# The order of the hand-over between stages: high-part passes first, sums in wide steps, nothing on GpSimd

## The chip, the cores and the metric

The kernel runs on one core of a Trainium2 chip. The time is the device time of one execution in microseconds (us); less is better. Three runs of the kernel before gave 1493.19, 1494.71 and 1496.35 us, median 1494.71.

## What is computed

A block of two transformer layers and a third, hybrid layer, for 256 tokens of width 1024 and 16 meta tokens put before them (272 tokens up to the last part of the second layer, 256 from there). In outline:

```python
for i in range(2):
    f1 = swiglu(rmsnorm(h, g[0]), w_gate, w_up, w_down);  h = h + 0.5 * rmsnorm(f1, g[1])
    m = attention(rmsnorm(h, g[2]));                       h = h + rmsnorm(m, g[3])   # neighborhood, then differential
    f2 = swiglu(rmsnorm(h, g[4]), ...);                    h = h + 0.5 * rmsnorm(f2, g[5])
x = x + rms_norm(concat(causal_attention, mlstm) @ w_out, g)    # its projections: rms_norm(x) @ w_in
x = x + rms_norm(square(relu(rms_norm(x, g) @ w_up)) @ w_down, g)
```

All is float32. Every stage is therefore the same in form: a norm of the residual h, products with large weights, some work between, a last product, and the norm of that added to h.

## The kernel before

h lies in SBUF with the features on the partitions, as eight blocks of 128 features by 272 tokens. Every product is made of three passes over parts in float32r: each weight chunk of 1024 by 128 is split in a high part `wh` and a low part `wl`, x in `xh` and `xl`, and TensorE adds `wh*xh + wh*xl + wl*xh` (`mm3`, lines 358 to 360). `gemm` makes one tile of 128 outputs: eight blocks of x, three matmuls each.

**Weights.** `Weights` streams raw chunks in by DMAs that SyncE issues (three buffers), `high()` copies a half to `wh` on ScalarE (L122), `low()` subtracts to `wl` (L134) on the engine that it is given, or else on `W.engine`, which is VectorE outside the mixers; when the second half of a raw chunk is through, the next load is issued. At most seven split chunks (`W_BUFS`) stand ready or in use. `pump(n)` makes up to n lows and highs; it is called behind every gemm.

**The end of a part.** `Post.evac` takes the eight last tiles: their squares into a sum, and `f = m*g`. `Post.finish` makes rstd: row sums on TensorE (L309, products with ones), a power on GpSimd (L314), and transposes back to columns (L333 to L338) into PSUM as `bc`. Then block j of the new residual is `h = h + f*bc`: `addend` (L561, `hb`, one operand in PSUM) and the addition (L567).

**The start of the next part.** `Norm` has x = h*g without rstd, which is applied behind the products: `block` makes `xh` on ScalarE (L401), `low` makes `xl` on VectorE (L411), `square` the squares on ScalarE (L344, L350, L352) and their sum `accp` on GpSimd (L353, L407). `head` makes the row sums of that sum and rstd, `tail` turns it (`rb`, L420); both run inside the second gemm behind the first tiles, `head` behind its block 0 and `tail` behind its block 3.

**The hand-over** is `start_phase`, called seven times: ahead of the three mixers, of three feed-forward parts, and of the last one (the first feed-forward has `first_phase`, with another order). While `finish` and its wait run, TensorE turns over on weights (`turn_over`, L433, two sets of nine). For blocks 0 and 1 `xh` is made straight from the addend (L442, from `old`, h*g of before, and `hb`), and h gets its addend beside that on GpSimd (L444). Then the first four tiles of the new stage are made together, block by block: for block k eight passes with `xh` (L455 and L456, L468 and L469) and four with `xl` (L459, L471), 96 matmuls in all; the low part of block k and the residual of block k + 2 stand in turn on VectorE, and two `W.pump(1, pool)` put two weight splits on GpSimd. Each engine works its queue in the order of the program.

Of the kernel before, what the change touches and what calls it, by code (L numbers as in the profile page):

```python
# [21 lines left out]
T = S + NM  # L22
# [51 lines left out]
class Weights:  # L74
    """Streams weight chunks [128, kb, 256] and splits each half of their columns into two
    float32r parts; of chunks with all their columns side by side, each half of their rows."""
# [64 lines left out]

    def pump(self, n=2, engine=None):
        ready = self.n_high
        for _ in range(n):
            if self.n_split < ready:
                self.low(engine)
            self.high()
        self.flush()
# [23 lines left out]
def block_kernel(ctx: ExitStack, tc: tile.TileContext, a, out):  # L172
# [25 lines left out]
    def keep_in(*slots):  # L198
        """The blocks that keep() hands out in turn during a mixer."""
        ring_blocks[:] = [t[:, j, :] for t in slots for j in range(t.shape[1])]  # L200
# [116 lines left out]
    def mean_head(acc, cols):  # L317
        """The mean of the squares, in rows of tokens."""
        p, m = ps_t((128, 4)), small([128, 4])
        n = row_sums(p, acc, cols)  # L320
        dve.tensor_scalar(m[:, 0:n], p[:, 0:n], 1.0 / D, EPS, op0=OP.mult, op1=OP.add)
        return m
# [18 lines left out]
    def square_into(acc, src, j, cols, bias=0.0, engine=dve):  # L341
        """The squares into the sum; the last block's stay beside it, for the product with ones."""
# [45 lines left out]
    class Norm:  # L388
        """x = h*g, split in two parts block by block; rstd is applied behind the products."""
# [18 lines left out]

        def low(self, j):
            c = self.cols  # L410
            dve.scalar_tensor_tensor(self.xl[:, j, c], h[:, j, c], self.g[:, j:j + 1],  # L411
                                     self.xh[:, j, c].bitcast(F32), op0=OP.mult, op1=OP.subtract)
# [10 lines left out]
    def start_phase(norm, post, n=4):  # L423
        """The first tiles, block by block of x as it comes.  The first two blocks of x are summed
        beside h, and the tensor engine turns over on weights while nothing is there for it."""
# [14 lines left out]
        t = [post.addend(k) for k in range(2)]  # L440
        for k in range(2):
            dve.scalar_tensor_tensor(norm.xh[:, k, c], t[k][:, c], norm.g[:, k:k + 1], old[k][:, c],  # L442
                                     op0=OP.mult, op1=OP.add)
            pool.tensor_tensor(h[:, k, c], h[:, k, c], t[k][:, c], op=OP.add)  # L444
        post.block(2)
        norm.block(2)
        norm.low(0)
        norm.low(1)
        post.block(3)
        norm.block(3)  # L450
        for k in range(2):
            norm.square(k)
        for k in range(2):
# [3 lines left out]
        for k in range(2):  # L457
            for q in range(n):
                pe.matmul(ps[q][:, c], w[q][0][:, k, :], norm.xl[:, k, c], start=False, stop=False)  # L459
        W.pump(1, pool)  # L460
        for k in range(2, 8):
            norm.low(k)
            if k + 2 < 8:
                post.block(k + 2)
                norm.block(k + 2)
            norm.square(k)
            for q in range(n):
                pe.matmul(ps[q][:, c], w[q][0][:, k, :], norm.xh[:, k, c], start=False, stop=False)  # L468
                pe.matmul(ps[q][:, c], w[q][1][:, k, :], norm.xh[:, k, c], start=False, stop=False)  # L469
            for q in range(n):  # L470
                pe.matmul(ps[q][:, c], w[q][0][:, k, :], norm.xl[:, k, c], start=False, stop=k == 7)  # L471
            if k == 5:
                W.pump(1, pool)
# [4 lines left out]
    def first_phase(norm, feed, n=4):  # L478
        """The first tiles of all: the passes in the order in which their operands come."""
# [53 lines left out]
    class Post:  # L533
        """The last products of a part: f = m*g beside the sum of squares, then h += f*rstd."""
# [96 lines left out]
    def proj_out(post, x, order=range(8)):  # L631
        """The product behind a mixer: the first four tiles block by block while the mixer ends."""
# [193 lines left out]
    def transpose_pair(dst, src):  # L826
        """[128, T] -> three token tiles, the last one with the last 16 tokens only."""
# [6 lines left out]
    class Ring:  # L834
        """Tiles of a mixer's turned weights, in the place of the residual's addend."""
# [10 lines left out]
    def softmax(ps, parts, n):  # L846
        """exp(logits - max) and 1/sum; the bias comes in parts of the columns."""
# [37 lines left out]
    def available(n):  # L885
        """Steps without work until the products have brought this unit's operands."""
# [200 lines left out]
    def token_rms(o):  # L1087
        """The sum of the squares of a token tile's 128 columns."""
# [422 lines left out]
    # the last product with the tokens on the partitions: out = h + (u @ w) * rstd * g  # L1511
# [90 lines left out]
```

## Time and profile before

| | |
|---|---|
| median of three runs | 1494.71 us |
| span of the profiled execution | 1495.0 us |
| TensorE busy | 1445.0 us (97%) |
| VectorE busy | 913.4 us (61%) |
| ScalarE busy | 753.9 us (50%) |
| GpSimd busy | 413.7 us (28%) |

PE is TensorE's matmuls, PEld its weight loads, DVE is VectorE, ACT is ScalarE, POOL is GpSimd. Records of neighbouring instructions can overlap, because the end of one is recorded after the next has begun: so the step from start to start, not the duration, tells the pace of a queue. A line in the timeline may stand for several like instructions in a row (x2), with the time from the first start to the last end; in brackets stand the idle time of the engine before it and what ended it.

### The profile page before, as it was taken

The page shows a single profiled execution, that of the slowest core. Times are in us where ns is not written, and L with a number is a line of the kernel's source. Part 1 is how long each engine was busy: PE and PEld are TensorE (multiplying, and loading weights), DVE is VectorE, ACT ScalarE, POOL GpSimd, SP SyncE. Part 2 cuts the span into 40 slices and gives each one's busy share as a digit, 9 for nine tenths or more (in the row PEclk, how much of TensorE's full clock was granted, in tenths as well). Part 3 has the DMA queues.
Part 4 walks back from the last instruction along what each step waited for, and adds up shares of the span by engine and source line. Part 5 has one row for each costly group of instructions (what it writes and reads, how often), then busy time and mean ns, then how long its engine had stood idle before and what let it go on. Part 6 is the DMA issues. An engine that isn't in the chain of part 4 may idle for free.

```text
span 1495.0 us, 27199 instructions
## 1 busy us (share of the span) xinstructions
PE 1445.0 (97%) x10996; PEld 1374.9 (92%) x10996; DVE 913.4 (61%) x1727; ACT 753.9 (50%) x1369; POOL 413.7 (28%) x300
## 2 busy tenths in 40 slices
PE   9999999899999999999999899999999898999998
PEld 8999998688899999999999798999999887999886
DVE  6777448853775544865545755675555667586542
ACT  5554445554664444554444565564444555576541
POOL 4324005452322100522102564232200855030000
PEclk9999999999999999999999999999999899999999
DMA  8896554432375555365553423276554533256651
GB/s 238 252 256 184 183 162 134 107 100 71 108 256 181 169 181 166 96 216 170 183 167 102 159 96 114 85 226 187 173 184 135 163 120 111 89 172 195 212 179 46
DMA packets 231708, 236.43 MB, mean 158 GB/s; under 512 B 17825, under 2 KB 221798, under 8 KB 231390
## 3 DMA queue, kind: packets, MB, share of 16 engines
q1 hardware_dynamic: 230750, 229.63, 49.2%
q0 software_dynamic: 688, 4.99, 1.1%
q8 instruction: 87, 1.43, 0.4%
q14 instruction: 39, 0.32, 0.1%
q10 hardware_dynamic: 144, 0.07, 0.0%
HBM read 233.60 MB, written 5.13 MB: 160 GB/s over the span
## 4 chain that ended last, share of the span: by engine, by line
PE 67%; DVE 7%; ACT 2%; issue 2%; POOL 1%; POOLq 0%; DVEq 0%; ACTq 0%
PE pm L358 18%; PE pm L360 18%; PE pm L359 18%; PE ps L1526 2%; PE ps L1525 2%; DVE xl L411 2%; PE ps L1527 2%; DVE h L567 1%; DVE hb L561 1%; PE ps L1129 1%; PE pt L309 1%; POOL accp L353 1%; PE ps L1101 1%; ACT wh L122 1%; PE ps L932 0%
## 5 line engine op out<-in xcount | busy, mean ns | idle before, releaser
L358 PE MATMUL pm<-xh,wh 128*128 128x272 f32 (+1 forms) x1992 | 584.4, 293 | 0.4 <-DVE s L851 0.4
L360 PE MATMUL pm<-xh,wl 128*128 128x272 f32 (+1 forms) x1992 | 572.6, 287 | 0.0
L359 PE MATMUL pm<-xl,wh 128*128 128x272 f32 (+1 forms) x1992 | 571.1, 287 | 0.0
L122 ACT ACTIVATE wh<-wr 128x1024 fp32r<-128x1024 f32 (+2 forms) x433 | 443.4, 1033 | 190.6 <-PE pm L359 119.4
L134 DVE TENSOR_TENSOR wl<-wr,wh 128x1024 fp32r<-128x1024 f32 (+1 forms) x354 | 444.7, 1262 | 130.4 <-ACT wh L122 129.5
L358 PEld LDWEIGHTS pm<-xh,wh 128*128 128x128 f32 x1992 | 378.6, 190 | 14.3 <-issue 11.1
L360 PEld LDWEIGHTS pm<-xh,wl 128*128 128x128 f32 x1992 | 378.3, 190 | 0.0
L359 PEld LDWEIGHTS pm<-xl,wh 128*128 128x128 f32 x1992 | 378.2, 190 | 0.1
L134 POOL TENSOR_TENSOR wl<-wr,wh 128x1024 fp32r<-128x1024 f32 x80 | 194.7, 2441 | 91.4 <-ACT wh L122 85.4
L360 PE MATMUL pm<-mh,wl 128*128 128x272 f32 (+1 forms) x704 | 202.3, 287 | 0.0
L358 PE MATMUL pm<-mh,wh 128*128 128x272 f32 (+1 forms) x704 | 202.1, 287 | 0.0
L359 PE MATMUL pm<-ml,wh 128*128 128x272 f32 (+1 forms) x704 | 201.5, 286 | 0.0
L594 POOL TENSOR_TENSOR sr<-sl,rb 128x272 f32<-128x272 f32 (+1 forms) x88 | 106.4, 1213 | 319.9 <-ACT sl L592 319.9
L360 PEld LDWEIGHTS pm<-mh,wl 128*128 128x128 f32 x704 | 132.7, 189 | 0.0
L358 PEld LDWEIGHTS pm<-mh,wh 128*128 128x128 f32 x704 | 132.6, 188 | 0.0
L359 PEld LDWEIGHTS pm<-ml,wh 128*128 128x128 f32 x704 | 132.6, 188 | 0.0
L314 POOL TENSOR_TENSOR s<-s,mhalf 128x3 f32<-128x3 f32 (+1 forms) x15 | 12.0, 799 | 386.0 <-DVE s L327 372.9
L385 ACT ACTIVATE mh<-m 128x272 fp32r<-128x272 f32 (+1 forms) x88 | 37.7, 428 | 120.4 <-DVE m L599 120.2
L599 DVE TENSOR_TENSOR m<-pm,sr 128x272 f32<-128x272 f32 (+1 forms) x88 | 38.2, 434 | 78.1 <-PE pm L360 70.5
L592 ACT ACTIVATE sl<-gq 128x272 f32<-128x272 f32 (+1 forms) x88 | 36.9, 428 | 87.9 <-DVE gq L590 87.5
L590 DVE TENSOR_TENSOR gq<-pm,rb 128x272 f32<-128x272 f32 (+1 forms) x88 | 37.5, 433 | 70.1 <-PE pm L360 62.2
L353 DVE TENSOR_TENSOR accf<-accf,sq 128x272 f32<-128x272 f32 (+1 forms) x42 | 18.3, 435 | 83.3 <-ACT sq L352 83.2
(345 smaller groups left out, 1998.9 us busy)
## 6 DMA issues: line engine op xcount, KB each, us to landing
wr<-in_ffn_w_gate_dram SPq DMA_DIRECT2D x43, 1024.0 KB
wr<-in_ffn_w_up_dram SPq DMA_DIRECT2D x43, 1024.0 KB
wr<-in_ffn_w_down_dram SPq DMA_DIRECT2D x32, 1024.0 KB
wr<-in_w_up_dram SPq DMA_DIRECT2D x16, 1024.0 KB
wr<-in_w_down_dram SPq DMA_DIRECT2D x16, 1024.0 KB
wr<-in_ffn_w_down_dram SPq DMA_DIRECT2D x16, 768.0 KB
wr<-in_na_w_qkv_dram SPq DMA_DIRECT2D x12, 1024.0 KB
wr<-in_da_w_qkv_dram SPq DMA_DIRECT2D x12, 1024.0 KB
```

The source lines that it names most:

```text
L122: self.nc.scalar.activation(hi, w, AF.Copy)
L134: engine.tensor_tensor(lo, w, hi.bitcast(F32), op=OP.subtract)
L353: engine.tensor_tensor(acc[:, cols], acc[:, cols], q[:, cols], op=OP.add)
L358: pe.matmul(ps, wh[:, k, :], xh[:, j, cols], start=start, stop=False)
L359: pe.matmul(ps, wh[:, k, :], xl[:, j, cols], start=False, stop=False)
L360: pe.matmul(ps, wl[:, k, :], xh[:, j, cols], start=False, stop=stop)
L385: act.activation(hi, src, AF.Copy)
L411: dve.scalar_tensor_tensor(self.xl[:, j, c], h[:, j, c], self.g[:, j:j + 1], self.xh[:, j, c].bitcast(F32), op0=OP.mult, op1=OP.subtract)
L590: dve.tensor_tensor(t[:, c], ps[:, c], norm.rb[:, c], op=OP.mult)
L592: act.activation(s[:, c], t[:, c], AF.Silu)
L594: pool.tensor_tensor(s2[:, c], s[:, c], norm.rb[:, c], op=OP.mult)
L599: dve.tensor_tensor(t[:, c], ps[:, c], gated.pop(f)[:, c], op=OP.mult)
```

## The change

In `start_phase` alone, with two small methods for it:

- The addends into h of blocks 0 and 1 go from GpSimd to VectorE, and behind the residual's other six blocks; `xh` of block 0 now stands ahead of the addend of block 1.
- VectorE makes the residual of all the blocks 2 to 7 before the first low part, then all eight low parts in a row. On TensorE all 64 passes with `xh` stand first and the 32 with `xl` behind.
- The squares are three wide instructions on ScalarE (blocks 2 to 5, 6 and 7, 0 and 1), into the place of the addends' factor f, with two weight copies (`W.high()`) between them. `Norm.sum` adds them on VectorE in three steps of 4, 2 and 1 blocks' width.
- The two weight splits that GpSimd had are `W.low_if()` on VectorE, one ahead of the sum and one behind it.

Comments and docstrings are taken out so that the line numbers stay.

```diff
+    def low_if(self):
+        if self.n_split < self.n_high:
+            self.low()
...
+        def sum(self, sq):
+            c = self.cols
+            dve.tensor_tensor(sq[:, 0:4, c], sq[:, 0:4, c], sq[:, 4:8, c], op=OP.add)
+            dve.tensor_tensor(sq[:, 0:2, c], sq[:, 0:2, c], sq[:, 2:4, c], op=OP.add)
+            dve.tensor_tensor(self.acc[:, c], sq[:, 0, c], sq[:, 1, c], op=OP.add)
...
-        t = [post.addend(k) for k in range(2)]
+        t = []
         for k in range(2):
+            t.append(post.addend(k))
             dve.scalar_tensor_tensor(norm.xh[:, k, c], t[k][:, c], norm.g[:, k:k + 1], old[k][:, c],
                                      op0=OP.mult, op1=OP.add)
-            pool.tensor_tensor(h[:, k, c], h[:, k, c], t[k][:, c], op=OP.add)
-        post.block(2)
-        norm.block(2)
-        norm.low(0)
-        norm.low(1)
-        post.block(3)
-        norm.block(3)
-        for k in range(2):
-            norm.square(k)
-        for k in range(2):
+        for k in range(2, 8):
+            post.block(k)
+            norm.block(k)
         for k in range(2):
+            dve.tensor_tensor(h[:, k, c], h[:, k, c], t[k][:, c], op=OP.add)
+        squares = post.f
+        for x, y in ((2, 6), (6, 8), (0, 2)):
+            act.activation(squares[:, x:y, c], h[:, x:y, c], AF.Square)
+            if x:
+                W.high()
+        for k in range(8):
+            norm.low(k)
+        for k in range(8):
             for q in range(n):
                 pe.matmul(ps[q][:, c], w[q][0][:, k, :], norm.xh[:, k, c], start=k == 0, stop=False)
                 pe.matmul(ps[q][:, c], w[q][1][:, k, :], norm.xh[:, k, c], start=False, stop=False)
-        for k in range(2):
-            for q in range(n):
-                pe.matmul(ps[q][:, c], w[q][0][:, k, :], norm.xl[:, k, c], start=False, stop=False)
-        W.pump(1, pool)
-        for k in range(2, 8):
-            norm.low(k)
-            if k + 2 < 8:
-                post.block(k + 2)
-                norm.block(k + 2)
-            norm.square(k)
-            for q in range(n):
-                pe.matmul(ps[q][:, c], w[q][0][:, k, :], norm.xh[:, k, c], start=False, stop=False)
-                pe.matmul(ps[q][:, c], w[q][1][:, k, :], norm.xh[:, k, c], start=False, stop=False)
+        for k in range(8):
             for q in range(n):
                 pe.matmul(ps[q][:, c], w[q][0][:, k, :], norm.xl[:, k, c], start=False, stop=k == 7)
-            if k == 5:
-                W.pump(1, pool)
+        W.low_if()
+        norm.sum(squares)
+        W.low_if()
         W.done(n)
         W.pump(2)
```

## Rows read from the trace of the kernel before

**Rows 1.** The page: span, and busy time (share of the span) and instructions by engine.

```profile
span 1495.0 us, 27199 instructions
PE 1445.0 (97%) x10996; PEld 1374.9 (92%) x10996; DVE 913.4 (61%) x1727; ACT 753.9 (50%) x1369; POOL 413.7 (28%) x300
```

**Rows 2.** Windows, product to row sums (one of seven): length, engines' busy, clock, DMA.

```profile
386.37:409.56 23.19, 20.79 (x158) 19.60 (x158) 17.59 (x27) 11.30 (x24) 14.26 (x12) 1.00 0.25 74
...
sum 157.56, PE 139.78 PEld 131.88 DVE 121.21 ACT 80.70 POOL 98.10; mean PE 19.97 PEld 18.84 DVE 17.32 ACT 11.53 POOL 14.01
```

**Rows 3.** Timeline of TensorE, hand-over from 386 us: start, length, line, tiles.

```profile
389.43 1.31 PE L433 MATMUL pm<-wh 128*128 128x256 f32 x9
391.32 0.39 PE L455 MATMUL pm<-xh,wh 128*128 128x272 f32 x1 [0.58 <-DVE xh L442]
...
399.85 0.77 PE L471 MATMUL pm<-xl,wh 128*128 128x272 f32 x4 [1.09 <-DVE xl L411]
...
405.37 0.28 PE L358 MATMUL pm<-xh,wh 128*128 128x272 f32 x1
...
408.40 0.29 PE L358 MATMUL pm<-xh,wh 128*128 128x272 f32 x1
...
409.56 0.83 PE L309 MATMUL pt<-ones,accp 128*128 128x1 f32 x6 [0.62 <-POOL accp L407]
```

**Rows 4.** Timeline of VectorE in the same hand-over.

```profile
389.62 0.79 DVE L561 TENSOR_TENSOR hb<-f,pt 128x272 f32<-128x272 f32 x2 [1.60 <-PE pt L335]
390.32 1.87 DVE L442 SCALAR_TENSOR_TENSOR xh<-hb,G,go 128x272 fp32r<-128x272 f32 x2
392.11 0.42 DVE L561 TENSOR_TENSOR hb<-f,pt 128x272 f32<-128x272 f32 x1
392.57 0.44 DVE L567 TENSOR_TENSOR h<-h,hb 128x272 f32<-128x272 f32 x1
392.93 0.91 DVE L411 SCALAR_TENSOR_TENSOR xl<-h,G,xh 128x272 fp32r<-128x272 f32 x2
...
397.26 2.53 DVE L411 SCALAR_TENSOR_TENSOR xl<-h,G,xh 128x272 fp32r<-128x272 f32 x1
...
404.67 3.38 DVE L134 TENSOR_TENSOR wl<-wr,wh 128x1024 fp32r<-128x1024 f32 x1 [0.77 <-ACT wh L122]
...
413.32 1.21 DVE L134 TENSOR_TENSOR wl<-wr,wh 128x1024 fp32r<-128x1024 f32 x1
```

**Rows 5.** Timeline of GpSimd in the same hand-over.

```profile
388.10 0.87 POOL L314 TENSOR_TENSOR s<-s,mhalf 128x3 f32<-128x3 f32 x1 [35.88 <-DVE s L327]
390.20 1.69 POOL L444 TENSOR_TENSOR h<-h,hb 128x272 f32<-128x272 f32 x2 [1.24 <-DVE hb L561]
...
396.91 2.58 POOL L134 TENSOR_TENSOR wl<-wr,wh 128x1024 fp32r<-128x1024 f32 x1
...
404.56 2.40 POOL L134 TENSOR_TENSOR wl<-wr,wh 128x1024 fp32r<-128x1024 f32 x1
```

**Rows 6.** Timeline of ScalarE in the same hand-over.

```profile
395.45 0.41 ACT L352 ACTIVATE sq<-h 128x272 f32<-128x272 f32 x1
...
396.72 0.51 ACT L401 ACTIVATE xh<-h,G 128x272 fp32r<-128x272 f32 x1
...
405.28 1.99 ACT L122 ACTIVATE wh<-wr 128x1024 fp32r<-128x1024 f32 x2
```

**Rows 7.** Timeline of TensorE, hand-over from 953 us (256 columns).

```profile
957.66 0.39 PE L455 MATMUL pm<-xh,wh 128*128 128x256 f32 x1 [0.59 <-DVE xh L442]
...
971.18 0.28 PE L358 MATMUL pm<-xh,wh 128*128 128x256 f32 x1
...
974.03 0.28 PE L358 MATMUL pm<-xh,wh 128*128 128x256 f32 x1
...
975.37 0.60 PE L309 MATMUL pt<-ones,accp 128*128 128x1 f32 x4 [0.83 <-POOL accp L407]
```

**Rows 8.** Timeline of TensorE inside a mixer (differential attention).

```profile
841.80 0.79 PE L1122 MATMUL pt<-ident,keep 128*128 128x128 f32 x3 [3.00 <-DVE keep L1113]
```

## The prediction

> **What bounds the kernel now.** TensorE is busy for 1445.0 of 1495.0 us [rows 1], so time can be won only where it waits for others or for its filler. I read the busy page first, then the windows of the seven places where `start_phase` hands one stage to the next, then one of them (from 386 us) engine by engine. Four hand-overs work on 272 columns (from 219.7, 386.4, 595.3 and 804.0 us), three on 256 (from 953.6, 1149.2 and 1298.9). Those of one kind are alike to within 0.25 us, so one stands for its kind. From the last product of the stage before to the row sums of the new x this one takes 23.19 us; all seven take 157.6 us, with GpSimd busy for 98.1 of them [rows 2]. The granted clock there is 1.00 (the 2.4 GHz level), so nothing in them is a clock's doing.
>
> Inside one [rows 3], TensorE loses time at three places. It starts on x at 391.32, when its filler (nine matmuls from 389.43, 1.31 us) has long ended, because `xh` of block 0 came late from VectorE. The 96 passes of the first four tiles, from 391.32 to the first gemm at 405.37, take 14.05 us; undisturbed matmuls have a pitch of (408.40 - 405.37) / 24 = 0.126 us, so 96 need 12.13 and 1.92 are lost, 1.09 of it in one idle at 399.85 that a low part of x ends. And the row sums start at 409.56: the second gemm's first three matmuls end their turn at 408.40 + 0.38 = 408.78, so 0.78 is lost to GpSimd's last addition.
>
> The VectorE rows [rows 4] say why. The same form, 272 columns, costs 0.49 us for a low part (0.91 for two) but 2.53 at 397.26, and 0.94 each for the two `xh` at 390.32; a weight split takes 1.21 at 413.32 but 3.38 at 404.67. Each long one lies under a GpSimd instruction [rows 5]: the additions into h from 390.20, the weight split 396.91 to 399.49, the one 404.56 to 406.96. The 2.53 one ends 0.31 us after GpSimd's split, the 3.38 one 1.09 after; each looks like its own short duration put behind GpSimd's. `hb`, which has one operand in PSUM, keeps its 0.42 to 0.43 throughout.
>
> A rule of the Trainium skill bears on the durations that I take below: "SBUF — State Buffer", section "Who interferes with whom", has a VectorE instruction with two SBUF inputs and a GpSimd instruction that reads SBUF exclude one another for a whole instruction, the later one waiting. The rows above agree. By that rule the short durations come back in full without GpSimd; were it shared bandwidth, they would as well, so the sum stays.
>
> **The change, part by part,** in the hand-over from 386 us.
>
> 1. *GpSimd is emptied.* Two h additions, seven square additions, two weight splits leave it; only the power for rstd (0.87 us, before and behind the crowded part) stays. VectorE then runs at its short durations.
>
> 2. *The first `xh`.* Addend 0 starts at 389.62 as before; a dependent instruction follows 0.46 later (392.11 to 392.57) [rows 4]; `xh` then takes 0.49, ends at 390.57, and TensorE starts some 0.05 later (before: 390.32 + 1.87 - 0.92 = 391.27, start 391.32), when its filler has just ended: 390.65. Gain 0.67.
>
> 3. *All high-part passes first.* VectorE's pitch per block is 0.46 + 0.36 = 0.82, ScalarE's `xh` takes 0.51 [rows 6]; TensorE wants a new block every 8 x 0.126 = 1.01. VectorE reaches block 2 at 389.62 + 0.46 + 0.42 + 0.46 + 0.42 = 391.38, h is there at 392.28, `xh` at 392.85, while TensorE is through two blocks at 392.67: a stall of about 0.2 (bounds 0 and 0.3), none later. The high passes end at 390.65 + 0.2 + 8.08 = 398.93. VectorE ends its six blocks at 391.38 + 4.92 = 396.30, the two h additions, which are new on it, at 397.02 (2 x 0.36), and low part 0 at 397.5; then one each 0.42, against four passes of 0.505. TensorE never waits for a low part. The passes end at 390.65 + 12.13 + 0.2 = 402.98: 12.33 instead of 14.05, gain 1.72.
>
> 4. *Weights.* At entry the fifth chunk behind x has its high part and no low part; the sixth and seventh have neither. The two highs stay on ScalarE (1.04 each), earlier than now. The fifth and sixth lows move from GpSimd to VectorE, 1.21 - 0.08 = 1.13 each in a row: fifth from 400.38 to 401.51, wanted by the third matmul of the first gemm, 402.98 + 0.25 = 403.23. What hides it is 1.7 us; without cover it would cost 1.13. SyncE's next load waits for the sixth low: 406.96 now, 405.1 then, so that queue is not later.
>
> 5. *Squares and their sum.* Sixteen short instructions (ScalarE 9, GpSimd 7) become three squares and three additions. ScalarE after the last `xh` (396.9): wide squares at the rate of its 1024-column copies, 1.04, to that of eight 0.41 squares, and two highs: 4.3 to 5.3 us, so it ends at 401.2 to 402.2. The additions, 1088, 544 and 272 columns, have no row of their own. From 0.43 at 272 and 1.21 at 1024 (1.04 ns a column) they are 1.28 + 0.71 + 0.43, 2.45 with the steps between; the other end is seven times a 0.44 addition, 3.08. Below nothing is excluded, for the work is new on VectorE. I take 2.45, as the 1024-column row is nearest. They end at 403.96 (404.6 to 405.3 at the far ends), and the row sums want them at 402.98 + 3.03 + 0.38 = 406.39: 1.1 to 2.4 us to spare. (At both far ends together the sixth low, next in the queue, would be 0.15 late.) Queued behind them on VectorE are the sixth low (to 405.09, wanted at 406.26), the seventh (406.22), and the mean behind the row sums (0.87 after they start, 407.26). So a new wait appears only if VectorE is some 1.1 us later than this. Gain of the row sums 0.78.
>
> Sum for 272 columns: 0.67 + 1.72 + 0.78 = 3.17. For 256 columns [rows 7]: the start 0.63 (0.67 x 256/272); pitch 2.85 / 24 = 0.119, 96 need 11.40, plus 0.2, against 971.18 - 957.66 = 13.52, gain 1.92; row sums at 974.03 + 0.36 = 974.39 instead of 975.37, gain 0.98; together 3.53. VectorE's work is 6% shorter there but for the weight splits; its margin at the sixth low falls to about 1.0. All: 4 x 3.17 + 3 x 3.53 = 23.3 us. Behind the row sums nothing changes: VectorE and ScalarE stand idle there now (the queue ends at 408.05) [rows 4] and then do, with as many chunks split. The profiled span of 1495.0 lies 0.3 above the median of the runs, 1494.71, and inside their spread, so nothing but the span counts: 1494.7 - 23.3 = **1471.4 us** (1.6% less).
>
> **The rivals.**
>
> *A mixer gives its part back.* Three hand-overs (219.7, 804.0, 1149.2) lead into attention, where TensorE later waits for other engines, as the 3.00 us at 841.80 for VectorE [rows 8]. Were these waits fixed by something that does not move with the row sums, such as a transfer, 3.17 + 3.17 + 3.53 = 9.9 us would go: 1481. For it: such waits are there. Against: their releasers are VectorE and ScalarE, whose chain begins with the row sums, and the load queue is not later. Chance 0.17.
>
> *VectorE becomes the bound, and it is slower.* All new work stands in one queue ahead of the row sums: 389.62 to 403.96, 14.3 us. It decides where this takes over 19.9 us (409.56 - 389.62, what the row sums have now), 5.6 us more. The wide instructions could do that: were the fifth split and the three additions, 1.13 + 2.45, stretched as the split at 404.67 was, 3.38 to 1.21 (2.8 times), they would take 6.4 us more, the row sums would come at 410.4, 0.8 later than now, and 7 x 0.8 = 5.6 us make 1500. Against: no GpSimd work is left to stretch them, and two short ones in a row take 0.79, less than twice 0.43. Chance 0.03; a stretch of half that, 3.2 us, of which 1 to 2.4 are covered, costs 7 x 0.8 to 2.2 of the gain: 1477 to 1487, 0.04.
> The Trainium skill has a rule that leads there: "VectorE: DVE Perf Modes", section "The DRAIN you can't avoid", puts a pipeline flush of about the duration less 266 ns behind every VectorE instruction. By that estimate the queue ahead of the row sums takes some 22.9 us, they come 3 us later than now, and the time is about 1516 us; the rows, with a step of 0.36 for a duration of 0.43, speak against it.
>
> *The change doesn't do what it says.* The long VectorE instructions wait for something else, and stay long. Then the start (0.67) is not won and low parts of 2.53 stay, but TensorE has eight blocks of high passes meanwhile: about half the sum, 1483; should the sums also be late, no change. Chance 0.03 and 0.03. The match of the four long instructions with GpSimd's speaks against it.
>
> **How the numbers follow.** Forecast 0.70 (1467 to 1476: 27.5 us won if the stall of 0.2 is absent and each of seven row sums gives 0.4 more behind it; some 19 if 0.6 of each comes back as small waits), mixers 0.17, half the stretch 0.04, half the sum 0.03, no change 0.03, slower 0.03. The range 1467 to 1481.5 leaves out about 0.17. A measurement of this kernel can tell about 0.2% (3 us): faster by that 0.93, within it 0.04, slower 0.03.
>
> **What would show it.** Right: in each hand-over low parts of 0.49 without exception, the first pass 0.67 earlier, no idle of TensorE inside the 96 passes but 0.2 at block 2, row sums without a wait, and the stage behind 3.2 to 3.5 us earlier; GpSimd some 90 us less busy (98.1 in the windows, of which its seven powers, 0.87 or less each, stay). Wrong: TensorE waiting for a weight split or a sum (step 4 or 5), long VectorE instructions without GpSimd (step 1), or longer waits in the mixers than the 3.00 of [rows 8].

## The result, and the profile after

Beside runs of the kernel before on the same chip (median 1495.14 us) the changed kernel took **1473.69 us** (1471.68 to 1474.20), a ratio of 0.9857 [0.9838, 0.9875]. In a later comparison (the run e11) it took 1473.34 against 1496.87 (0.9846 [0.9831, 0.9861]). The forecast was 1471.4, its range 1467 to 1481.5.

Line numbers of the changed file behind the new methods differ from those of the kernel before: L362 to L364 are the three products of `mm3`, L313 the row sums, L445 the filler, L566 and L572 addend and addition, L405 and L422 `xh` and `xl`, L455 `xh` of blocks 0 and 1, L461 their additions into h, L471 and L472 the high passes, L475 the low ones, L464 the wide squares, L416 to L418 their sum. Some runs below shift them by a few lines again; the tiles tell what is what.

The page after, span and busy engines; then windows of hand-overs, from the last product of the stage before to the row sums, as in [rows 2] (columns as there; one of 272 columns, one of 256, and the sum of all seven).

```profile
span 1472.4 us, 27036 instructions
PE 1438.7 (98%) x10996; PEld 1373.3 (93%) x10996; DVE 907.2 (62%) x1776; ACT 752.8 (51%) x1327; POOL 321.1 (22%) x223
```

```profile
383.82:403.94 20.12, 20.05 (x158) 19.44 (x158) 16.64 (x34) 11.07 (x18) 0.86 (x1) 1.00 0.23 71
...
941.60:960.02 18.42, 18.29 (x151) 17.83 (x152) 15.78 (x34) 10.56 (x18) 0.70 (x1) 1.00 0.21 67
...
sum 135.37, PE 134.62 PEld 130.74 DVE 113.88 ACT 79.13 POOL 5.55; mean PE 19.23 PEld 18.68 DVE 16.27 ACT 11.30 POOL 0.79
```

The seven windows lost 157.56 - 135.37 = 22.19 us [rows 2], and the span 1495.0 - 1472.4 = 22.6 [rows 1]. So nearly the whole gain lies in the hand-overs; the mixers between gave nothing back. TensorE now stands idle for 0.75 us of the seven windows together (135.37 - 134.62), and GpSimd works 5.55 us there instead of 98.1: only the powers are left.

TensorE in the hand-over that answers to [rows 3], 2.55 us earlier on the clock of the profile (386.37 - 383.82):

```profile
386.76 1.31 PE L445 MATMUL pm<-wh 128*128 128x256 f32 x9
388.05 0.39 PE L471 MATMUL pm<-xh,wh 128*128 128x272 f32 x1
388.28 0.29 PE L472 MATMUL pm<-xh,wl 128*128 128x272 f32 x1
388.40 0.29 PE L471 MATMUL pm<-xh,wh 128*128 128x272 f32 x1
...
390.05 0.29 PE L472 MATMUL pm<-xh,wl 128*128 128x272 f32 x1
390.39 0.40 PE L471 MATMUL pm<-xh,wh 128*128 128x272 f32 x1
390.62 0.29 PE L472 MATMUL pm<-xh,wl 128*128 128x272 f32 x1
...
396.52 4.18 PE L475 MATMUL pm<-xl,wh 128*128 128x272 f32 x32
400.54 0.29 PE L362 MATMUL pm<-xh,wh 128*128 128x272 f32 x1
...
403.94 0.72 PE L313 MATMUL pt<-ones,accp 128*128 128x1 f32 x6
```

The first pass follows the filler at once, the 32 low passes are one row without a wait, and so are the row sums. What is left is one small wait at block 2 (390.05 to 390.39). VectorE and ScalarE in the same place, answering to [rows 4, 6]:

```profile
386.95 0.44 DVE L566 TENSOR_TENSOR hb<-f,pt 128x272 f32<-128x272 f32 x1 [1.59 <-PE pt L339]
387.49 0.50 DVE L455 SCALAR_TENSOR_TENSOR xh<-hb,G,go 128x272 fp32r<-128x272 f32 x1
...
393.82 0.79 DVE L461 TENSOR_TENSOR h<-h,hb 128x272 f32<-128x272 f32 x2
394.52 3.38 DVE L422 SCALAR_TENSOR_TENSOR xl<-h,G,xh 128x272 fp32r<-128x272 f32 x8
397.83 1.21 DVE L134 TENSOR_TENSOR wl<-wr,wh 128x1024 fp32r<-128x1024 f32 x1
398.96 1.28 DVE L416 TENSOR_TENSOR f<-f 128x1088 f32<-128x1088 f32 x1
400.28 0.73 DVE L417 TENSOR_TENSOR f<-f 128x544 f32<-128x544 f32 x1
401.04 0.45 DVE L418 TENSOR_TENSOR accp<-f 128x272 f32<-128x272 f32 x1
401.39 2.36 DVE L134 TENSOR_TENSOR wl<-wr,wh 128x1024 fp32r<-128x1024 f32 x2
```

```profile
394.37 1.10 ACT L464 ACTIVATE f<-h 128x1088 f32<-128x1088 f32 x1
...
397.81 0.64 ACT L464 ACTIVATE f<-h 128x544 f32<-128x544 f32 x1
```

Eight low parts take 3.38 us in a row; the split is 1.21 long, not 3.38; ScalarE's last square ends at 398.45, half a microsecond before VectorE starts to add.

For 256 columns, TensorE's first pass, first product behind the passes, and row sums, answering to [rows 7]:

```profile
945.14 0.39 PE L471 MATMUL pm<-xh,wh 128*128 128x256 f32 x1
...
956.87 0.28 PE L362 MATMUL pm<-xh,wh 128*128 128x256 f32 x1
...
960.02 0.50 PE L313 MATMUL pt<-ones,accp 128*128 128x1 f32 x4
```

### The profile page after: what moved, and what is told of

It is laid out like the page before. It is cut to its first block, busy times and chain, and to the rows that moved or that the text cites. A ratio compares the mean times of both kernels' runs of the same rounds, so it can differ in the third digit from the quotient of the medians.

```text
span 1472.4 us, 27036 instructions
## 1 busy us (share of the span) xinstructions
PE 1438.7 (98%) x10996; PEld 1373.3 (93%) x10996; DVE 907.2 (62%) x1776; ACT 752.8 (51%) x1327; POOL 321.1 (22%) x223
## 4 chain that ended last, share of the span: by engine, by line
PE 74%; DVE 4%; ACT 1%; issue 0%; POOL 0%; DVEq 0%; POOLq 0%; ACTq 0%
PE pm L362 19%; PE pm L364 19%; PE pm L363 19%; PE ps L1531 2%; PE ps L1530 2%; PE ps L1532 2%; PE pm L475 2%; PE pm L471 1%; PE pm L472 1%; PE ps L1134 1%; PE pt L313 1%; PE ps L1106 1%; PE ps L937 0%; PE pm L445 0%; DVE hb L566 0%
## 5 line engine op out<-in xcount | busy, mean ns | idle before, releaser
L362 PE MATMUL pm<-xh,wh 128*128 128x272 f32 (+1 forms) x1992 | 584.2, 293 | 0.4 <-DVE s L856 0.4
L364 PE MATMUL pm<-xh,wl 128*128 128x272 f32 (+1 forms) x1992 | 572.1, 287 | 0.0
L134 DVE TENSOR_TENSOR wl<-wr,wh 128x1024 fp32r<-128x1024 f32 (+2 forms) x368 | 446.4, 1221 | 123.9 <-ACT wh L122 123.0
L362 PEld LDWEIGHTS pm<-xh,wh 128*128 128x128 f32 x1992 | 378.3, 190 | 14.1 <-issue 10.9
L364 PEld LDWEIGHTS pm<-xh,wl 128*128 128x128 f32 x1992 | 378.0, 190 | 0.0
L364 PE MATMUL pm<-mh,wl 128*128 128x272 f32 (+1 forms) x704 | 202.2, 287 | 0.0
L362 PE MATMUL pm<-mh,wh 128*128 128x272 f32 (+1 forms) x704 | 202.1, 287 | 0.0
L134 POOL TENSOR_TENSOR wl<-wr,wh 128x1024 fp32r<-128x1024 f32 x66 | 159.9, 2430 | 91.7 <-ACT wh L122 79.8
L364 PEld LDWEIGHTS pm<-mh,wl 128*128 128x128 f32 x704 | 132.6, 188 | 0.0
L362 PEld LDWEIGHTS pm<-mh,wh 128*128 128x128 f32 x704 | 132.5, 188 | 0.0
```

The source lines that it names most:

```text
L134: engine.tensor_tensor(lo, w, hi.bitcast(F32), op=OP.subtract)
L362: pe.matmul(ps, wh[:, k, :], xh[:, j, cols], start=start, stop=False)
L364: pe.matmul(ps, wl[:, k, :], xh[:, j, cols], start=False, stop=stop)
```

## The experiments

The theory was that VectorE's long instructions were held by GpSimd, that the order of passes fits TensorE to VectorE's pace, and that all else on VectorE lies under it. Each ratio is to runs of the kernel before beside it. The last column is the sum of the seven windows, as above, in each run's profile. It decides more than the median, for outside the windows the mixers vary: in e2, e4, e5 and e6t the first mixer took 2.4 to 2.7 us longer than in the changed kernel, in e2, e4, e5 and e10 the third 2.0 to 2.3 shorter, each with another granted clock (last section).

| kernel | median us | ratio to before | seven windows |
|---|---|---|---|
| before | 1494.71 | | 157.56 |
| changed | 1473.69 | 0.9857 [0.9838, 0.9875] | 135.37 |
| e1: old order, GpSimd emptied | 1536.61 | 1.0267 [1.0243, 1.0290] | 196.92 |
| e10: the same, additions one block later | 1487.91 | 0.9940 [0.9923, 0.9957] | 153.21 |
| e2: changed, splits on GpSimd | 1483.72 | 0.9921 [0.9901, 0.9940] | 146.03 |
| e3: changed, two additions on GpSimd | 1482.17 | 0.9913 [0.9897, 0.9929] | 143.60 |
| e6t: changed, two idle multiplies on GpSimd | 1485.95 | 0.9938 [0.9917, 0.9958] | 146.63 |
| e6m: changed, four idle fills on GpSimd | 1475.26 | 0.9865 [0.9843, 0.9887] | 135.31 |
| e4: changed, sum in narrow steps | 1475.54 | 0.9864 [0.9843, 0.9884] | 138.32 |
| e5: changed, old order of passes | 1486.67 | 0.9941 [0.9922, 0.9959] | 148.31 |
| e9: e5, both splits ahead of the sum | 1478.27 | 0.9890 [0.9872, 0.9908] | 140.09 |
| e8, e12: changed, addends ahead | 1469.77, 1469.73 | 0.9823 [0.9805, 0.9840], 0.9817 [0.9803, 0.9830] | 133.98, 133.73 |
| e11: changed, beside e12 | 1473.34 | 0.9846 [0.9831, 0.9861] | 135.26 |

### What GpSimd's work costs VectorE

Weight splits back on GpSimd:

```diff
-        W.low_if()
+        W.low_if(pool)   # both places
```

> The changed kernel with its two moved weight splits of each hand-over given back to GpSimd; order, wide sums and h additions stay. Theory (a two-input GpSimd instruction holds up VectorE's two-input ones): the first split starts right behind the power, at about the time of the first xh, which comes about 1.2 us later; the second runs 2.4 us beside the low parts, one of which takes 2.5 instead of 0.49 and costs TensorE about 0.5; together 1.7 us a hand-over, 1485.6 us (1482 to 1489). Rival (the order alone makes the gain, GpSimd beside it is harmless): 1473 to 1475, and VectorE ends its queue 2.3 us earlier.

Measured: 1483.72, 10.0 us above the changed kernel. GpSimd and VectorE at the first `xh`:

```profile
388.50 2.37 POOL L134 TENSOR_TENSOR wl<-wr,wh 128x1024 fp32r<-128x1024 f32 x1
...
389.73 1.44 DVE L455 SCALAR_TENSOR_TENSOR xh<-hb,G,go 128x272 fp32r<-128x272 f32 x1
```

The split ends at 390.87, `xh` at 391.17. The other split holds one of the low parts, and the eight take 5.53 us in a row instead of 3.38:

```profile
397.69 5.53 DVE L422 SCALAR_TENSOR_TENSOR xl<-h,G,xh 128x272 fp32r<-128x272 f32 x8
```

Next, only the two short additions into h:

```diff
             dve.scalar_tensor_tensor(norm.xh[:, k, c], ...)
+            pool.tensor_tensor(h[:, k, c], h[:, k, c], t[k][:, c], op=OP.add)
...
-        for k in range(2):
-            dve.tensor_tensor(h[:, k, c], h[:, k, c], t[k][:, c], op=OP.add)
```

> The changed kernel, with the additions into h of blocks 0 and 1 again on GpSimd beside the first two steps that make xh. Theory (a GpSimd instruction that reads SBUF and a VectorE instruction with two SBUF operands keep one another out): GpSimd's additions, 0.84 us each in the kernel before, hold up xh of block 1 and the additions into h of blocks 2 and 3 on VectorE; the first pass starts as in the changed kernel or up to 0.3 us later, block 2 is 0.3 to 0.8 us late, and 0.2 to 0.7 us a hand-over are lost: 1475 to 1479 us, against 1473.7. The rival (only the two weight splits on GpSimd, long instructions, disturb anybody): no VectorE instruction in the hand-over is longer than 0.6 us and the time is 1473.7.

Measured: 1482.17, more than expected. VectorE and GpSimd, block 0:

```profile
388.70 1.10 DVE L455 SCALAR_TENSOR_TENSOR xh<-hb,G,go 128x272 fp32r<-128x272 f32 x1
388.74 0.77 POOL L457 TENSOR_TENSOR h<-h,hb 128x272 f32<-128x272 f32 x1 [1.24 <-DVE hb L565]
```

I had thought that `xh`, first in the queue, would go first. Its record does begin first, by 0.04 us, but it ends 0.30 after GpSimd's 389.51: it waited. Both `xh` take 1.1, the first pass comes 0.59 later and the passes, which now wait at block 1 too, take 0.54 more: 1.13 to 1.26 us a hand-over for two additions of 0.77. So a short instruction that GpSimd starts beside the critical one costs as much as a long one elsewhere: the split of 2.4 us beside the low parts lengthened the passes by 0.35 to 0.68 (e2).

To separate GpSimd's use of SBUF from any result that VectorE might have waited for, two runs add work on a scratch tile that nothing else touches, behind the power:

```diff
+    scratch = cp.tile([128, 1024], F32, name="scratch")
...
         post.finish(turn_over)
+        for _ in range(2):
+            pool.tensor_tensor(scratch, scratch, scratch, op=OP.mult)   # e6t
+        for _ in range(4):
+            pool.memset(scratch, 1.0)                                   # e6m, instead
```

> The changed kernel, and added to it, in each hand-over behind the power for rstd, two multiplies of 128 x 1024 on GpSimd whose operands and result lie in a scratch tile that nothing else uses: no instruction waits for them, and nothing is left out. Theory (exclusion for a whole instruction): each takes about 2.4 us, the first runs under the first xh and the second under the next VectorE instructions with two SBUF operands; the first xh takes some 1.5 us instead of 0.5, another instruction some 2 us, the first pass starts about 1 us later and block 2 is late again: 2 to 3.5 us a hand-over, 1488 to 1498 us. Rival (the long VectorE instructions waited for a result or a buffer of GpSimd's, not for its use of SBUF): no VectorE instruction is longer than in the changed kernel, 1473.7 us.

> The changed kernel, and added to it, in each hand-over behind the power for rstd, four fills of a scratch tile of 128 x 1024 with a constant on GpSimd: GpSimd is as busy in the same place as with the two multiplies, writes SBUF and reads nothing from it; nothing is left out. Theory (what keeps VectorE out is GpSimd's reading of two operands): VectorE's instructions keep their durations (0.49 us xh, 0.36 to 0.42 the additions) under the fills, 1473.7 us within 2. Rival (any use of SBUF by GpSimd does it): the first xh is held up as with the multiplies, 1 us or more a hand-over, 1480 us or more.

Measured: 1485.95 with the multiplies (below the expected 1488, for they took 1.89 and 1.97 us and not 2.4), 1475.26 with the fills, whose windows are those of the changed kernel (135.31). The multiplies, then the fills, each with the `xh` under them:

```profile
394.09 1.60 DVE L459 SCALAR_TENSOR_TENSOR xh<-hb,G,go 128x272 fp32r<-128x272 f32 x1
...
391.45 3.94 POOL L454 TENSOR_TENSOR scratch<-scratch 128x1024 f32<-128x1024 f32 x2
```

```profile
390.21 0.50 DVE L459 SCALAR_TENSOR_TENSOR xh<-hb,G,go 128x272 fp32r<-128x272 f32 x1
...
388.98 3.98 POOL L454 MEMSET scratch<- 128x1024 f32 x4
```

Nothing waits for the scratch tile, yet `xh` ends at 395.69, 0.30 us after the second multiply (395.39); under 3.98 us of fills it keeps its 0.50. So GpSimd holds VectorE without any result between them, and not by being busy or by writing SBUF: the multiplies read SBUF, the fills don't. (The two differ in kind as well; a GpSimd instruction that reads only one operand was not run.)

The section "Who interferes with whom" of the Trainium skill's page "SBUF — State Buffer" draws the same line: a VectorE instruction with two SBUF inputs contends with a GpSimd instruction that reads SBUF, not with one that only writes it. The two runs agree with it.

### What the order is worth without GpSimd

The kernel before, with GpSimd's additions and splits on VectorE at the same places:

```diff
-            pool.tensor_tensor(h[:, k, c], h[:, k, c], t[k][:, c], op=OP.add)
+            dve.tensor_tensor(h[:, k, c], h[:, k, c], t[k][:, c], op=OP.add)
...
-            norm.square(k)
+            norm.square(k, dve)
...
-        W.pump(1, pool)
+        W.pump(1)
```

> The kernel before with its own order; only the work that GpSimd had in the hand-over (two additions into h, seven additions of squares, two weight splits) is put on VectorE at the same places. Theory (GpSimd stretches VectorE's two-input instructions, but the old order puts the extra work ahead of low parts that TensorE waits for): all low parts take 0.49 us and splits 1.21, the first pass comes 0.4 us earlier, the row sums need not wait (0.8), but the 96 passes take about 15 us instead of 14.05, for TensorE waits about 1.1 us twice for the low part behind a split; net 0.3 us a hand-over, 1493 us (1490 to 1496). Rival A (the stretch is all, the order nothing): nearly the whole gain, 1474 to 1478. Rival B (order is all, the stretch nothing): low parts of 2.5 us stay, time as before or above, 1495 to 1505.

Measured: 1536.61, 2.7% slower than before and 44 us from what I expected, though every low part takes 0.49. ScalarE, VectorE and TensorE within one block:

```profile
403.38 0.43 DVE L561 TENSOR_TENSOR hb<-f,pt 128x272 f32<-128x272 f32 x1
...
403.85 0.44 DVE L567 TENSOR_TENSOR h<-h,hb 128x272 f32<-128x272 f32 x1
...
404.32 0.52 ACT L401 ACTIVATE xh<-h,G 128x272 fp32r<-128x272 f32 x1 [1.94 <-DVE h L567]
...
404.75 0.41 ACT L352 ACTIVATE sq<-h 128x272 f32<-128x272 f32 x1
...
405.20 0.44 DVE L353 TENSOR_TENSOR accp<-accp,sq 128x272 f32<-128x272 f32 x1 [0.91 <-ACT sq L352]
...
405.97 0.43 DVE L561 TENSOR_TENSOR hb<-f,pt 128x272 f32<-128x272 f32 x1
```

VectorE's addition of a square waits for ScalarE's square, which stands behind the next block's `xh`, which waits for VectorE's h: the two wait in turn, 2.59 us a block (403.38 to 405.97, addend to addend), where TensorE needs 12 x 0.126 = 1.51. On GpSimd that addition held nobody's queue. TensorE's idle times then cost its clock as well. Windows of 5 us (columns as above):

```profile
410.00:415.00 5.00, 2.25 (x16) 1.80 (x14) 3.68 (x8) 2.87 (x8) 0.00 (x0) 1.00 0.00 0
415.00:420.00 5.00, 4.99 (x27) 4.99 (x28) 2.21 (x4) 1.89 (x2) 0.00 (x0) 0.66 0.90 285
```

TensorE was busy for 2.25 of the 5 us up to 415; behind them the granted clock is 0.66, some two thirds of the time at 1.2 GHz. If the mutual wait is the cause, breaking it without taking work away must give most of this back:

```diff
+        def square_late(self, j):
...
+            act.activation(q[:, c] if j else self.acc[:, c], h[:, j, c], AF.Square)
+            for late in self.__dict__.pop("late", []):
+                dve.tensor_tensor(self.acc[:, c], self.acc[:, c], late[:, c], op=OP.add)
+            if j:
+                self.late = [q]
...
-            norm.square(k, dve)
+            norm.square_late(k)
```

> As the run e1_old_order_no_gpsimd (the order of the kernel before, GpSimd's additions and weight splits on VectorE at the same places; 1536.61 us), with one difference: VectorE adds the square of a block one block later, behind the addition into h that ScalarE waits for, so that ScalarE and VectorE don't wait for one another in turn. Theory (the loss of that run was this mutual wait: 2.59 us a block, where TensorE needs 1.51): VectorE's queue is then the limit, per block a low part, an addend, an addition into h and an addition of squares, 0.41 + 0.36 + 0.47 + 0.36 = 1.6 us, with two weight splits of 1.14 us between; some 5.5 blocks of 1.0 us less, less what TensorE's clock had lost besides, 5 to 7 us a hand-over: 1488 to 1502 us. Rival (the loss was the amount of work on VectorE, or the clock alone): 1520 us or more.

Measured: 1487.91, at the lower end of what I expected; 6.2 us a hand-over came back ((196.92 - 153.21) / 7). So in the old order, with a workable queue, emptying GpSimd is worth 4.4 us of the 22.2. What it lacks against the changed kernel, 2.5 us a hand-over, are mainly idle times of TensorE of 0.50 and 0.95 us for low parts behind the two splits in VectorE's queue, and VectorE at 1.6 us a block against TensorE's 1.51:

```profile
395.56 0.78 PE L482 MATMUL pm<-xl,wh 128*128 128x272 f32 x4 [0.50 <-DVE xl L422]
...
403.05 0.77 PE L482 MATMUL pm<-xl,wh 128*128 128x272 f32 x4 [0.95 <-DVE xl L422]
```

From the other side, the changed kernel with the order of passes and low parts of before (the squares wide and the splits where the change has them):

```diff
+        post.block(2)
+        norm.block(2)
+        norm.low(0)
+        norm.low(1)
...
+        for k in range(2, 8):
+            norm.low(k)
+            if k + 2 < 8:
+                post.block(k + 2)
+                norm.block(k + 2)
...
         W.low_if()
         norm.sum(squares)
         W.low_if()
```

> The changed kernel with the old order of passes and low parts (block by block: eight high passes, four low ones; low part of block k ahead of the residual of block k + 2), nothing on GpSimd, wide squares and sum and both splits behind all low parts. Theory (with VectorE at its short durations, 1.24 us a block against TensorE's 1.51, the order matters only at the start): TensorE waits about 0.9 us once, for the low part of block 0, and saves the 0.2 at block 2: about 0.65 us a hand-over more than the changed kernel, 1478 us (1476 to 1481). Rival A (high passes first are the core of the change): two or more idles, 1.5 us or more a hand-over, 1484 us or more. Rival B (the order gives nothing): 1473 to 1475.

Measured: 1486.67, 8.7 above what I expected. The time is that of rival A, but not its reason: the passes have one idle, at the low part of block 0, and are only 0.54 us longer. VectorE ahead of the sum, then TensorE in the second gemm:

```profile
405.49 1.29 DVE L416 TENSOR_TENSOR f<-f 128x1088 f32<-128x1088 f32 x1 [2.35 <-ACT f L484]
```

```profile
409.20 0.39 PE L364 MATMUL pm<-xh,wl 128*128 128x272 f32 x1 [0.85 <-DVE wl L134]
```

h is complete only towards the end of the passes, so ScalarE begins the squares 10.58 us after the first addend (401.37 less 390.79), in the changed kernel 7.42 (394.37 less 386.95). VectorE's queue stands for 2.35 us before the sum, and the sixth split behind it comes too late for TensorE. To see that it is this split and not the late row sums:

```diff
         W.low_if()
-        norm.sum(squares)
         W.low_if()
+        norm.sum(squares)
```

> The changed kernel with the order of passes and low parts of the kernel before, as in the run e5_old_pass_order (1486.67 us), but both weight splits stand ahead of the sum of squares on VectorE. In that run VectorE waited 2.35 us for ScalarE's last square, and the split behind the sum came 1.0 to 1.4 us too late for TensorE. Theory (the loss beyond the passes is this split, queued behind the waiting sum): TensorE's wait at the low part of the second gemm goes; what is left is the 0.54 us in the passes and whatever the row sums wait for the sum, 0.6 to 1.2 us a hand-over, 1478 to 1482 us. Rival (it is the late row sums, or the passes themselves, that cost it): 1485 to 1487 us, as there.

Measured: 1478.27, as expected: the wait is gone. With 272 columns only 0.53 to 0.57 us a hand-over are lost against the changed kernel, all in the passes; with 256 the window loses 0.80 to 0.88, 0.54 to 0.59 of it in the passes, and the stage behind it some 0.35 more, for the sum and with it the power come late. So "all high parts first" pays little in the passes themselves: of the 12.9 us that e5 loses in the windows (148.31 - 135.37), 3.8 are passes. The other 9.1 are won by completing h early, so that squares, highs and sum lie under the low parts. But that is one way of two: e9 gets 8.2 of them back in the old order by the place of one split.

### The sum, and what is left

Eight narrow squares and seven narrow additions instead of three wide ones each:

```diff
-            dve.tensor_tensor(sq[:, 0:4, c], sq[:, 0:4, c], sq[:, 4:8, c], op=OP.add)
...
+            dve.tensor_tensor(self.acc[:, c], sq[:, 2, c], sq[:, 3, c], op=OP.add)
+            for k in (4, 5, 6, 7, 0, 1):
+                dve.tensor_tensor(self.acc[:, c], self.acc[:, c], sq[:, k, c], op=OP.add)
...
-            act.activation(squares[:, x:y, c], h[:, x:y, c], AF.Square)
+            for k in range(x, y):
+                act.activation(squares[:, k, c], h[:, k, c], AF.Square)
```

> The changed kernel with its squares block by block (eight instructions on ScalarE) and their sum block by block (seven additions on VectorE), at the same places. Theory (the wide steps lie under cover): the sum ends about 1 us later, 403.9 less 1.5 stays enough ahead of the row sums, time 1473.7 us within 1.5. Rival (the wide steps carry a part of the gain): TensorE waits for the row sums or the sixth split 0.5 us or more in each hand-over, 1477 us or more.

Measured: 1475.54, between the two expectations; the windows are 2.95 us longer. VectorE, then TensorE, in a hand-over of 256 columns:

```profile
958.69 3.07 DVE L418 TENSOR_TENSOR accp<-accp,f 128x256 f32<-128x256 f32 x6
```

```profile
962.96 0.38 PE L364 MATMUL pm<-xh,wl 128*128 128x256 f32 x1 [0.38 <-DVE wl L134]
```

Each addition needs the one before, at 0.53 us a step ((3.07 - 0.42) / 5), 3.6 us in all instead of 2.4, and the sixth split behind is late for TensorE: the row sums come 0.6 us later. With 272 columns it costs 0.2. So 1.2 us more use up the margin of 1.0 to 1.2 that the prediction gave the sixth split.

The last wait, at block 2, is VectorE's chain of dependent steps. Addends one or two blocks ahead:

```diff
-        t = []
+        t = [post.addend(0)]
         for k in range(2):
-            t.append(post.addend(k))
             dve.scalar_tensor_tensor(norm.xh[:, k, c], ...)
+            if k == 0:
+                t += [post.addend(1), post.addend(2)]
         for k in range(2, 8):
-            post.block(k)
+            dve.tensor_tensor(h[:, k, c], h[:, k, c], t[k][:, c], op=OP.add)
             norm.block(k)
+            while len(t) < min(8, k + 3):
+                t.append(post.addend(len(t)))
```

> The changed kernel, with the addends made one to two blocks ahead of their use on VectorE, so that an instruction seldom follows at once the one whose result it needs: addend 0, xh of block 0, addends 1 and 2, xh of block 1, addition of block 2, and so on. Theory (the 0.21 to 0.27 us that TensorE waits at block 2 are VectorE's chain: two steps of 0.54 us from an addend to its xh and 0.47 to the addition into h, instead of 0.36 to 0.42): h of block 2 comes some 0.3 us earlier, the wait at block 2 falls below 0.1 us, nothing else moves, 0.1 to 0.25 us a hand-over: 1472 to 1473 us. Rival (VectorE has less to spare behind than it seems, the longer queue of addends delays a later block): another wait inside the passes, no gain.

Measured: 1469.77, better than expected, so both kernels were run once more side by side:

> The changed kernel itself, beside the next run on the same chip, since the 1473.69 us of the changed kernel and the 1469.77 of the run e8_addends_ahead come from different calls. Both theories: 1473.7 us within 1.5; its seven hand-overs take the same time as in its first profile within 0.1 us each.

> The kernel of the run e8_addends_ahead again. Theory (only what the traces of the hand-overs show is the order's doing: 0.12 to 0.24 us each, 1.4 in all; the other 2.8 us of the difference between the two spans lie in the mixers and come and go): 1.4 us under the changed kernel of this call, within 1.5, which the times can hardly tell. Rival (the mixers, too, gain by it): 3 to 5 us under it.

Measured: 1473.34 (1471.39 to 1476.50) and 1469.73 (1468.19 to 1469.94): 3.6 us, and the rival was right that more than the hand-overs gain. (The seven windows of e11 are each within 0.06 us of those in the first profile, as expected.) VectorE now makes h of block 2 earlier:

```profile
387.10 0.50 DVE L454 SCALAR_TENSOR_TENSOR xh<-hb,G,go 128x272 fp32r<-128x272 f32 x1
387.52 0.78 DVE L569 TENSOR_TENSOR hb<-f,pt 128x272 f32<-128x272 f32 x2
388.21 0.49 DVE L454 SCALAR_TENSOR_TENSOR xh<-hb,G,go 128x272 fp32r<-128x272 f32 x1
388.63 0.43 DVE L459 TENSOR_TENSOR h<-h,hb 128x272 f32<-128x272 f32 x1
```

The addition into h (L459) starts 1.53 us after the first `xh` (387.10), in the changed kernel 1.85 (389.34 less 387.49); TensorE waits no more at block 2, and the windows are 135.37 - 133.73 = 1.64 us shorter. Most of the rest lies in the third mixer, which takes 121.7 and 121.6 us in the two profiles of this version and 124.0 and 123.9 in those of the changed kernel; what differs in it is TensorE's clock. Windows of its first 20 us behind the second gemm, of the kernel before, the changed one, and this one:

```profile
1174.40:1194.40 20.00, 16.72 (x106) 16.41 (x106) 12.91 (x35) 10.85 (x16) 18.43 (x9) 0.74 0.59 169
```

```profile
1155.40:1175.40 20.00, 16.68 (x108) 16.36 (x107) 13.14 (x37) 10.85 (x16) 18.62 (x9) 0.74 0.66 199
```

```profile
1153.50:1173.50 20.00, 16.70 (x130) 16.46 (x129) 12.76 (x41) 12.91 (x20) 19.76 (x9) 0.91 0.62 185
```

TensorE is busy equally long, but makes 130 matmuls instead of 108, since less of the time passes at 1.2 GHz. Why a hand-over that is 0.24 us shorter changes this was not found. The shorter third mixer is not shown to be this order's own: e2, e4, e5 and e10 have it as well, though their hand-overs are longer than the changed kernel's. This version beats the kernel before by 1.8%, and the changed one by some 0.25% (1469.73 against 1473.34).

## Why the prediction was right, step by step

In the hand-over of [rows 3], with 2.55 us added to the times after, so that both stand on the clock of before:

| event | predicted | measured |
|---|---|---|
| first pass | 390.65 | 390.60 |
| wait at block 2 | 0.2 | 0.21 |
| last addition into h ends | 397.02 | 397.16 |
| first low pass | 398.93 | 399.07 |
| last square ends | 401.2 to 402.2 | 401.00 |
| fifth split | 400.38 to 401.51 | 400.38 to 401.59 |
| sum of squares ends | 403.96 | 404.04 |
| passes end | 402.98 | 403.09 |
| row sums | 406.39 | 406.49 |

**Steps 1 and 2** held: no long VectorE instruction is left in the hand-overs, and the first pass came 0.55 to 0.72 us earlier. That 390.65 was met so closely is partly luck, for two errors cancel: `xh` started 0.54 behind its addend and not 0.46, but the addend itself came 0.12 earlier than taken (389.50 on the clock of before, not 389.62). In e1, which empties GpSimd but makes both addends ahead of the first `xh`, the first pass came 0.31 to 0.57 earlier; the rest is the place of that `xh`. The runs e2, e3 and e6t show the cause, GpSimd instructions that read SBUF; e6m excludes that GpSimd's mere activity does it.

**Step 3** is the term that was mis-sized: the 96 passes gained 1.55 to 1.58 us and not 1.72 (256 columns: 1.79, not 1.92). They last 400.54 - 388.05 = 12.49 instead of 12.33. I charged the wait at block 2, but not that the matmul behind a wait is followed only 0.23 later, not 0.126 (388.05 to 388.28, 390.39 to 390.62): 0.10 twice. That is 0.13 to 0.17 a hand-over, nearly all of what the windows fell short. Of its mechanism, e5 and e9 show that the passes are the lesser part. What I had written as cover for steps 4 and 5, h complete early, is what the order mainly buys as long as a split stands behind the sum.

**Steps 4 and 5** held with what they claimed for margins: no split and no sum is waited for. The sum took 2.53 us against 2.45 taken, 1088 columns 1.28 as estimated from the 1024-column row. The far end of 3.08 was too low a bound: seven narrow additions took 3.7 us at 272 columns, since each depends on the one before. e4 and e5 show how thin the cover is: 1.2 us more on VectorE ahead of the sixth split, and TensorE waits for it.

**The sum**: 2.95 to 3.07 us a hand-over with 272 columns, where I had 3.17, and 3.38 to 3.43 with 256, where I had 3.53: 22.2 us in the windows and 0.4 outside them (22.6 - 22.2), against 23.3. The rest of the 2.3 us between 1471.4 and 1473.69 lies within the runs' spread: in the later comparison the medians differ by 23.5. The prediction set the span of 1495.0 beside the median of 1494.71, but a run's time lies above its span (1474.20 for 1472.4, 1.8 us), so that profile is of a run some 2 us above the median. As only the difference counts, the sum stands.

**The rivals.** From the row sums to the next hand-over the three mixers took 0.09, 0.18 and 0.36 us less than before, so none gave its part back. VectorE did not become the bound. A flush behind every VectorE instruction does not show: independent instructions of 0.43 to 0.50 follow one another every 0.35 to 0.41 us, and dependent ones after 0.47 to 0.55. The Trainium skill's page "VectorE: DVE Perf Modes", section "The DRAIN you can't avoid", from which I took that rival, also says that a next instruction which is not held back until the earlier ones have finished starts earlier; the prediction had left this out. What I had not among the rivals is what e1 ran into: emptying GpSimd alone, in the old order, makes the kernel slower by 2.7%, as two queues wait for each other. The prediction priced "no GpSimd" by durations and would have missed that, had the change not moved the sum behind the blocks.

## What to carry to other kernels

When work goes from a free engine to a busy one, first follow what it waits for and who stands behind it in that queue; durations say little if two queues wait in turn. An order that completes a shared operand early can be worth more by what it lets other engines do under the rest than by the waits it removes. Beside a critical VectorE instruction with two SBUF operands start no GpSimd addition, subtraction or multiply on SBUF, however short.

## What the runs showed of the hardware

- A VectorE instruction with two SBUF operands that begins under a GpSimd `tensor_tensor` ends a fixed time after it: 0.30 us with 272 columns (e2, e3, e6t, and the low part at 397.26 of [rows 4, 5]), 0.28 with 256, 1.08 to 1.09 with 1024. This holds even where its record begins 0.04 us before GpSimd's (e3); low parts that began 0.12 to 0.43 us before kept their length (in the kernel before). The addend, with one operand in PSUM, kept 0.40 to 0.44 under all of them.
- Two operands are not needed. In the first mixer of the kernel before, a `tensor_scalar` with one tensor operand in SBUF takes 0.36 us alone, but 2.30 here, under a GpSimd split from 260.40 to 262.76, and ends 0.16 after it:

```profile
260.62 2.30 DVE L910 TENSOR_SCALAR keep<-keep,s 128x272 f32<-128x272 f32 x1
```

- A matmul that follows a wait is followed by the next after 0.23 us (0.22 to 0.23 at 256 columns), against 0.126 (0.119) otherwise, with the granted clock at 1.00.
- The granted clock of one stage varied between profiles, and its time with it. From the row sums to the next hand-over the third mixer took 127.4 to 128.0 us where its granted clock was 0.95 (before, both of the changed kernel, e1, e3), 126.1 to 127.0 at 0.96 (e6t, e6m, e9) and 125.1 to 125.4 at 0.97 (e2, e4, e5, e8, e10, e12); the first mixer took 143.5 to 143.7 at 0.99, 144.5 to 145.0 at 0.98 (e1, e3) and 146.0 to 146.3 at 0.96 or 0.97 (e2, e4, e5, e6t). The largest of these differences exceed what the order of addends gained in all seven hand-overs.
